# Another opening for a two-layer decoder trunk: the first two tiles' modulation on TensorE, c turned from eight rows

## The chip, the core and the metric

The kernel runs on one NeuronCore of a Trainium2 chip. Its engines are TensorE (PE, matrix products into PSUM; its weight loads are a row of their own, PEld), VectorE (DVE), ScalarE (ACT), GpSimd (POOL) and SyncE (SP, which only issues transfers). Each engine runs its own queue in order, and semaphores join them. The metric is the device time of one execution in microseconds (us); lower is better.

## The reference, cut to what matters

```python
def rmsnorm(x, g):                       # over the 1024 channels
    return x * rsqrt(mean(x * x) + EPS) * g

for i in range(2):                       # x is (256 tokens, 1024), c is (1024)
    mod = silu(c) @ w_ada[i] + b_ada[i]  # six pieces of 1024: shift, scale, gate, twice
    h = rmsnorm(x, norm_mix[i]) * (1 + sc1) + sh1
    x = x + g1 * mixer_i(h)              # i = 0: dilated attention, 1: gated linear attention
    h = rmsnorm(x, norm_ffn[i]) * (1 + sc2) + sh2
    x = x + g2 * conv_ffn(h)
return rmsnorm(x, norm_final)
```

The attention's first step is `h @ w_in` (1024 to 9216). Its scores get a learnt bias per distance (`rel_bias`), which the kernel calls position terms.

## The kernel before, in words

Channels lie on partitions: x is eight tiles (`kt`) of 128 channels by 256 tokens. Products keep near float32 precision by splitting each operand into a rounded high part and the rest: `whi`, `wlo` of weights (ACT copies the high part, `low_part` on DVE makes the rest) and `hhi`, `hlo` of h; each product is three (`hhi,whi`, `hlo,whi`, `hhi,wlo`).

The opening does this. c arrives as one row (`c_row`); PE multiplies it with a column of ones, so that it stands on all partitions, and ACT's Silu leaves it in `c_bc`. The squares of x are added on DVE and ACT, and PE's product with `ones_d` (tile `ms`) gives the mean for the norm (`rstd_of`). For each tile `kt` the loop at `w0, h = [], []` loads 128 rows of the modulation's weights twice over (`ada_load`), DVE takes two dot products with `c_bc` (`ada_dot`, tiles `dot`; L142), ACT adds the bias (`mod`), `normed` makes `hhi` and `hlo`, and `split` and `low_part` the parts of `w0[kt]`, the columns of `w_in` for the first two pairs of heads. PE then runs 36 products of 256 columns and 6 of 384 per tile into `pqk` and `pv` (L696, L700, L203 to L205). Products of the position terms (`rows`, L409) and warm-ups (`keep_warm`, results unused) stand before the first tile on PE.

The order on each engine follows `behind(...)` (issue after the named instructions) where it is written out, and a scheduler elsewhere. Loads go through SP in program order into four `raw` buffers, so a load can start when its buffer's last reader is done. After the first projection come the attention of eight pairs of heads (weights `wv`, `wqk`; bias rows read back from `rows_d`), its output, the FFN and the second layer; the change leaves them as they are.

```python
    rows_ps, at = [], 0
    with behind(norm_ops[0]):
        keep_warm(3)
...
            last_row = mm(ps, tab[:, 16 * g : 16 * g + 16], oh[:33, c], start=True, stop=True)
            at += n
    with behind(last_row):
        keep_warm(6)
```

## Time and profile before

| | us |
|---|---|
| median of 3 runs | 748.4 (748.07 to 750.87) |
| the profiled execution | 752.01 |
| its span, first to last instruction | 750.2 |
| PE busy in the span | 741.7 (99%) |
| DVE, ACT, POOL busy | 648.2, 480.6, 31.7 |
| mean granted clock of PE | 0.998 |

The span is what the trace covers; 1.8 us of the profiled execution lie around it. An engine's busy time counts an instruction from its start to its end, so overlapping products on PE count once. In the rows further down a line such as L142 is a line of the kernel, out<-in names tiles, and a bracket at the end tells how long the engine was idle before it and what released it.

### The profile page before, as it was taken

The page shows a single profiled execution, that of the slowest core. Times are in us where ns is not written, and L with a number is a line of the kernel's source. Part 1 is how long each engine was busy: PE and PEld are TensorE (multiplying, and loading weights), DVE is VectorE, ACT ScalarE, POOL GpSimd, SP SyncE. Part 2 cuts the span into 40 slices and gives each one's busy share as a digit, 9 for nine tenths or more (in the row PEclk, how much of TensorE's full clock was granted, in tenths as well). Part 3 has the DMA queues.
Part 4 walks back from the last instruction along what each step waited for, and adds up shares of the span by engine and source line. Part 5 has one row for each costly group of instructions (what it writes and reads, how often), then busy time and mean ns, then how long its engine had stood idle before and what let it go on. Part 6 is the DMA issues. An engine that isn't in the chain of part 4 may idle for free.

```text
span 750.2 us, 15928 instructions
## 1 busy us (share of the span) xinstructions
PE 741.7 (99%) x6344; PEld 726.6 (97%) x6344; DVE 648.2 (86%) x1195; ACT 480.6 (64%) x943; POOL 31.7 (4%) x57
## 2 busy tenths in 40 slices
PE   8999999999999999999999999999999999999997
PEld 5999999999999999999999999999999999999996
DVE  6997998989988859999998886898969999997592
ACT  5556775555656658776766565865768766666551
POOL 0002001101101010000000000000010000000100
PEclk9999999999999999999999999999999999999999
DMA  9998789888788438877746997776757766874621
GB/s 349 399 304 294 241 317 369 270 315 280 263 309 284 132 117 295 311 281 240 256 128 207 315 341 243 256 266 224 261 194 274 281 223 236 211 179 157 205 100 57
DMA packets 39481, 187.20 MB, mean 250 GB/s; under 512 B 9020, under 2 KB 11708, under 8 KB 25838
## 3 DMA queue, kind: packets, MB, share of 16 engines
q1 hardware_dynamic: 39024, 185.73, 71.4%
q8 instruction: 50, 0.82, 0.4%
q10 hardware_dynamic: 382, 0.45, 0.2%
q14 instruction: 25, 0.20, 0.1%
HBM read 185.06 MB, written 1.10 MB: 248 GB/s over the span
## 4 chain that ended last, share of the span: by engine, by line
PE 98%; DVE 1%; ACT 0%; DMA 0%; issue 0%; DVEq 0%; ACTq 0%
PE pab L204 10%; PE pab L205 10%; PE pab L203 10%; PE pqk L203 6%; PE pqk L205 6%; PE pqk L204 6%; PE pd L204 5%; PE pd L205 5%; PE pd L203 5%; PE pv L203 4%; PE pv L205 4%; PE pv L204 4%; PE pqk L696 2%; PE py L203 2%; PE py L205 2%; PE py L204 2%
## 5 line engine op out<-in xcount | busy, mean ns | idle before, releaser
L176 ACT CAST whi<-raw 128x1024 fp32r<-128x1024 f32 (+4 forms) x264 | 237.8, 945 | 107.0 <-PE pab L204 55.0
L182 DVE TENSOR_TENSOR wlo<-raw,whi 128x1024 fp32r<-128x1024 f32 (+5 forms) x248 | 263.8, 1092 | 30.6 <-ACT whi L176 29.8
L205 PE MATMUL pab<-hhi,wlo 128*128 128x256 f32 x672 | 185.0, 276 | 0.0
L204 PE MATMUL pab<-hlo,whi 128*128 128x256 f32 x672 | 184.9, 277 | 0.0
L203 PE MATMUL pab<-hhi,whi 128*128 128x256 f32 x672 | 183.1, 277 | 0.0
L204 PEld LDWEIGHTS pab<-hlo,whi 128*128 128x128 f32 x672 | 126.1, 188 | 0.2
L205 PEld LDWEIGHTS pab<-hhi,wlo 128*128 128x128 f32 x672 | 126.2, 188 | 0.0
L203 PEld LDWEIGHTS pab<-hhi,whi 128*128 128x128 f32 x672 | 125.1, 188 | 0.1
L142 DVE CUSTOM_DVE_ANT_0 ada_raw<-ada_raw,c_bc 128x1024 f32<-128x1024 f32 x96 | 114.3, 1230 | 4.6 <-DMA ada_raw<-in_w_ada 4.4
L203 PE MATMUL pqk<-hhi,whi 128*128 128x256 f32 x374 | 102.4, 279 | 0.0
L204 PE MATMUL pqk<-hlo,whi 128*128 128x256 f32 x374 | 101.8, 277 | 0.0
L205 PE MATMUL pqk<-hhi,wlo 128*128 128x256 f32 x374 | 101.3, 278 | 0.0
L205 PE MATMUL pd<-ghi,wlo 128*128 128x256 f32 x308 | 84.9, 276 | 0.0
L204 PE MATMUL pd<-glo,whi 128*128 128x256 f32 x308 | 84.9, 276 | 0.0
L203 PE MATMUL pd<-ghi,whi 128*128 128x256 f32 x308 | 84.7, 276 | 0.0
L203 PEld LDWEIGHTS pqk<-hhi,whi 128*128 128x128 f32 x374 | 69.9, 188 | 0.2
L204 PEld LDWEIGHTS pqk<-hlo,whi 128*128 128x128 f32 x374 | 69.9, 188 | 0.0
L205 PEld LDWEIGHTS pqk<-hhi,wlo 128*128 128x128 f32 x374 | 69.2, 188 | 0.1
L204 PEld LDWEIGHTS pd<-glo,whi 128*128 128x128 f32 x308 | 57.8, 188 | 0.0
L205 PEld LDWEIGHTS pd<-ghi,wlo 128*128 128x128 f32 x308 | 57.8, 188 | 0.0
L203 PEld LDWEIGHTS pd<-ghi,whi 128*128 128x128 f32 x308 | 57.7, 188 | 0.0
L204 PE MATMUL pv<-wlo,hhi 128*128 128x384 f32 (+2 forms) x160 | 52.8, 332 | 0.0
(272 smaller groups left out, 1440.8 us busy)
## 6 DMA issues: line engine op xcount, KB each, us to landing
raw<-in_w_up SPq DMA_DIRECT2D x42, 1024.0 KB, 4.9
ada_raw<-in_w_ada SPq DMA_DIRECT2D x29, 1024.0 KB, 6.0
raw<-in_w_down SPq DMA_DIRECT2D x28, 704.0 KB, 5.1
ada_raw<-in_w_ada SPq DMA_DIRECT2D x38, 512.0 KB, 6.8
raw<-in_wqk SPq DMA_DIRECT2D x18, 1024.0 KB, 6.7
raw<-in_wv SPq DMA_DIRECT2D x14, 768.0 KB, 7.0
raw<-in_w SPq DMA_DIRECT2D x7, 960.0 KB, 6.1
raw<-in_w_v_b SPq DMA_DIRECT2D x6, 768.0 KB, 5.0
```

Of the source, the lines that this page charges most:

```text
L142: i = dotted[0] = nc.vector.tensor_tensor_reduce(w, w, c_bc, op0=ALU.mult, op1=ALU.add, scale=1.0, scalar=0.0, accum_out=dot,)
L176: copied[0] = nc.scalar.copy(part(hi[:, c]), part(raw[:, c]))
L182: last_lo[0] = nc.vector.tensor_tensor(part(lo[:, c]), part(raw[:, c]), part(hi[:, c].bitcast(F32)), op=ALU.subtract)
L203: mm(ps, a[0], b[0], start=start, stop=False)
L204: mm(ps, a[0], b[1], start=False, stop=False)
L205: return mm(ps, a[1], b[0], start=False, stop=stop)
L696: mm(pqk[i], w[a], h[kt][b], start=s and i % 2 == 0 and (a, b) == (0, 0), stop=e and i % 2 == 1 and b == 1)
```

## The change

c is loaded as eight rows of 128, PE turns it (tile `ct`), and ACT's Silu puts it into column 0 of each 32-column block of a zeroed tile (`c_sel`). DVE and POOL each multiply four copies of the identity with four of these columns (`spread`), and a product with `ones_d` gives c on all partitions, which ACT copies to `c_bc`. For tiles 0 and 1 the modulation is now made by PE: eight products per tile, each with one block of `c_sel` as 32 columns of weights and 256 columns of `ada_first` passing through, in four column groups (`first_products`); DVE copies the four groups' sums out (`first_parts`), and two one-column products add them and turn them (`first_sums`). The position terms are six products of 128 columns in column groups of one bank. h's unrounded value of tiles 1 to 7 comes from `scaled_x` (x times the norm, on DVE for three and four tiles at once) and an ACT instruction. The two small tables `rel_bias` and `onehot` are loaded from POOL's queue. PE's order over the tiles is written out (`front`, `front_values`, `back`).

```diff
--- before.py
+++ after.py
-    c_row = wspl.tile([P, 2048], F32, tag="whi", name="c_row")
-    nc.scalar.dma_start(c_row[:1, :D], I["c"])
+    oh = wspl.tile([P, 2048], F32, tag="whi", name="oh")
+    c_sel, c_rows = oh[:, D + T : D + 2 * T].rearrange("p (k j) -> p k j", k=KT), oh[:KT, D : D + P]
+    nc.scalar.dma_start(c_rows, I["c"])
+    ident = const.tile([P, P], F32, name="ident")
+    make_identity(nc, ident)
+    nc.gpsimd.memset(c_sel, 0.0)
...
-    nc.scalar.dma_start(tab[:32, :], I["rel_bias"])
+    nc.gpsimd.dma_start(tab[:32, :], I["rel_bias"])
...
-    oh = wspl.tile([P, 2048], F32, tag="whi", name="oh")
-    nc.scalar.dma_start(oh[:33, :NROW], I["onehot"])
+    nc.gpsimd.dma_start(oh[:33, :NROW], I["onehot"])
...
     nc.vector.memset(eps, EPS)
-    ident = const.tile([P, P], F32, name="ident")
-    make_identity(nc, ident)
+    one = eps_one[:, 1:2]
+    nc.vector.memset(one, 1.0)
...
+    def keep_warm(n, tag="p"):
+        ps = bank("warm", tag)
+        for i in range(n):
+            last = mm(ps[:, :P], ones_d, ones_d, start=True, stop=True)
+        return last
     c_bc = const.tile([P, D], F32, name="c_bc")
-    for n in range(2):
-        ps = bank("cb", "t")
-        last_c = mm(ps, ones_d[:1, :], c_row[:1, 512 * n : 512 * n + 512], start=True, stop=True)
-        silu = nc.scalar.activation(c_bc[:, 512 * n : 512 * n + 512], ps, AF.Silu, scale=float(D))
+    first_warm = keep_warm(4)
+    nc.scalar.activation(eps_one[:, 2:3], one, AF.Silu)
+    c_turned = bank("ct", "s")
+    with behind(first_warm):
+        last_turn = nc.tensor.transpose(c_turned[:, 0:KT], c_rows, ident[:KT, :KT])
+    silu = nc.scalar.activation(c_sel[:, :, 0], c_turned[:, 0:KT], AF.Silu)
+    exp_ln_after(silu)
+    with behind(last_turn):
+        last_warm = keep_warm(4)
+    spread = wspl.tile([P, 2048], F32, tag="wlo", name="spread")
+    for n, engine in enumerate((nc.vector, nc.gpsimd)):
+        c = slice(512 * n, 512 * n + 512)
+        engine.tensor_tensor(spread[:, c].rearrange("p (k j) -> p k j", j=P),
+                             ident.unsqueeze(1).to_broadcast([P, 4, P]),
+                             c_sel[:, 4 * n : 4 * n + 4, 0:1].to_broadcast([P, 4, P]), op=ALU.mult)
+    c_ps = []
+    with behind(last_warm):
+        for n in range(2):
+            c_ps.append(bank("cb", "t"))
+            last_c = mm(c_ps[n], ones_d, spread[:, 512 * n : 512 * n + 512], start=True, stop=True)
+    with behind(last_c):
+        last_c = keep_warm(3)
...
+    def first_load(kt):
+        raw = wraw.tile([P, 2048], F32, tag="raw", name="ada_raw")
+        for c in (slice(0, D), slice(D, 2 * D)):
+            nc.sync.dma_start(raw[:, c], I["ada_first"][kt][:, c])
+        return raw
+    def first_products(raw, ps, ks, *after):
+        for k in ks:
+            j = slice(32 * (k % 4), 32 * (k % 4) + 32)
+            with behind(*after):
+                last = mm(ps[j, 0:T], c_sel[:, k, :], raw[:, T * k : T * k + T], start=(k < 4), stop=(k >= 4))
+        return last
+    def first_parts(ps, *after):
+        part = tmp.tile([P, T], F32, tag="sqacc", name="part")
+        with behind(*after):
+            i = nc.vector.tensor_copy(part, ps[:, 0:T])
+        return part, i
+    def first_sums(kt, ps, part, *after):
+        for i in range(2):
+            with behind(*after):
+                last = mm(ps[:, T + i : T + i + 1], part[:, P * i : P * i + P], one, start=True, stop=True)
+        return last, [modulation(0, piece, kt, ps[:, T + i : T + i + 1]) for i, piece in enumerate((1, 0))]
...
+    FIRST = 2
     sq = wspl.tile([P, 2048], F32, tag="wlo", name="sq").rearrange("p (k t) -> p k t", k=KT)
+    firsts = [first_load(0)]
+    for i in (0, 2):
+        nc.vector.tensor_tensor(sq[:, i : i + 2, :], x_all[:, i : i + 2, :], x_all[:, i : i + 2, :], op=ALU.mult)
+    last_add = nc.vector.tensor_tensor(sq[:, 0:2, :], sq[:, 0:2, :], sq[:, 2:4, :], op=ALU.add)
+    for i in (4, 6):
+        last_sq = nc.scalar.activation(sq[:, i : i + 2, :], x_all[:, i : i + 2, :], AF.Square)
+    with behind(last_add):
+        last_add = nc.vector.tensor_tensor(sq[:, 4:6, :], sq[:, 4:6, :], sq[:, 6:8, :], op=ALU.add)
+    with behind(last_sq):
+        for n in range(2):
+            last_copy = nc.scalar.activation(c_bc[:, 512 * n : 512 * n + 512], c_ps[n], AF.Copy, scale=float(D))
+    with behind(last_add):
+        last_terms = scale_terms(0)
+    mean, dots = bank("ms", "p"), bank("dots", "s")
     with behind(last_c):
-        keep_warm(4)
...
+        for i in (0, 1, 4, 5):
+            last_c = mm(mean[:, :T], ones_d, sq[:, i, :], start=(i == 0), stop=(i == 5))
+    for ks in (range(4), range(4, KT)):
+        last_c = first_products(firsts[0], dots, ks, last_c)
+    with behind(last_c):
+        last_warm = keep_warm(1)
...
+    part, last_part = first_parts(dots, last_terms)
+    def scaled_x(a, b, *after):
+        with behind(*after):
+            return nc.vector.tensor_tensor(all_early[:, a:b, 0:T], x_all[:, a:b, :],
+                                           r.unsqueeze(1).to_broadcast([P, b - a, T]), op=ALU.mult)
+    last_part = scaled_x(1, 4, last_part)
+    last_dots, last_mods = first_sums(0, dots, part, last_warm)
 
     rows_ps, at = [], 0
-    with behind(norm_ops[0]):
-        keep_warm(3)
-        for i, (g, n) in enumerate(ROWS):
-            c = slice(at, at + n)
-            ps = bank("rows", "t")[:16, 0:n]
+    row_bank = bank("rows", "t")
+    for i, (g, n) in enumerate(ROWS):
+        for first in range(0, n, P):
+            c = slice(at, at + P)
+            j = len(rows_ps)
+            ps = row_bank[32 * (j % 4) : 32 * (j % 4) + 16, P * (j // 4) : P * (j // 4) + P]
             rows_ps.append((ps, c))
-            last_row = mm(ps, tab[:, 16 * g : 16 * g + 16], oh[:33, c], start=True, stop=True)
-            at += n
-    with behind(last_row):
-        keep_warm(6)
+            with behind(last_dots):
+                last_row = mm(ps, tab[:, 16 * g : 16 * g + 16], oh[:33, c], start=True, stop=True)
+            at += P
...
+    def front(kt, terms, tiles=range(2 * NG), *after):
+        s, e = kt == 0, kt == KT - 1
+        for a, b in terms:
+            for i in tiles:
+                w = w0_parts(kt, P * i)
+                with behind(*after):
+                    last = mm(pqk[i], w[a], h[kt][b], start=s and i % 2 == 0 and (a, b) == (0, 0), stop=e and i % 2 == 1 and (a, b) == terms[-1])
+        return last
+    def front_values(kt, terms, *after):
+        s, e = kt == 0, kt == KT - 1
+        wv = w0_parts(kt, 6 * P, NG * P)
+        for a, b in terms:
+            for t in range(2):
+                with behind(*after):
+                    last = mm(pv[t][:, : NG * P], h[kt][a][:, P * t : P * t + P], wv[b], start=s and (a, b) == (0, 0), stop=e and (a, b) == BOTH[-1])
+        return last
+    def back(kt, tiles, *after):
+        for i in tiles:
+            with behind(*after):
+                last = mm3(pqk1[i], w0_parts(kt, 9 * P + P * i), h[kt], kt == 0 and i % 2 == 0, kt == KT - 1 and i % 2 == 1)
+        return last
...
     w0, h = [], []
-    last = last_add
+    last = last_part
     for kt in range(KT):
...
+        if kt >= FIRST:
+            ada = ada_load(0, kt)
+            with behind(last):
+                dots = [ada_dot(0, kt, 0, ada)]
+            with behind(dots[0][0]):
+                dots.append(ada_dot(0, kt, 1, ada))
+        elif kt:
+            firsts.append(first_load(kt))
+        if kt:
+            w0.append(split(I["w0"][kt], 15 * P, after=((), ()) if kt < FIRST else ((dots[0][1],), ()), lows=False))
+        else:
+            raw = wraw.tile([P, 2048], F32, tag="raw", name="raw")
+            for c in (slice(0, 960), slice(960, 1920)):
+                nc.sync.dma_start(raw[:, c], I["w0"][0][:, c])
+            whi = wspl.tile([P, 2048], F32R, tag="whi", name="whi")
+            wlo = wspl.tile([P, 2048], F32R, tag="wlo", name="wlo")
+            copied[0] = last_mods[1]
+            for c in (slice(0, 384), slice(384, 960), slice(960, 1920)):
+                with behind(copied[0]):
+                    copied[0] = nc.scalar.copy(whi[:, c], raw[:, c])
+            w0.append((whi, wlo, raw, 960))
+        hi, lo = h_hi[kt], h_lo[kt]
         if kt == 0:
+            a, sh = mod[0, 1, 0], mod[0, 0, 0]
+            hf = tmp.tile([P, T], F32, tag="xr", name="xr")
+            with behind(last):
+                nc.vector.scalar_tensor_tensor(hf, x[0], a[:, 0:1], r, op0=ALU.mult, op1=ALU.mult)
+            nc.vector.tensor_scalar(hi, hf, sh[:, 0:1], None, op0=ALU.add)
+            last = nc.vector.scalar_tensor_tensor(lo, hf, sh[:, 0:1], hi[:, :].bitcast(F32), op0=ALU.add, op1=ALU.subtract)
+            for i in range(2):
+                with behind(last):
+                    last = low_part(w0[0], i)
+            h.append((hi, lo))
             with behind(copied[0]):
                 for ps, c in rows_ps:
                     nc.scalar.copy(rows[:, c], ps)
+            done = front(0, ((0, 0), (0, 1)), range(2 * NG), last_row)
+            done = front_values(0, ((0, 0), (1, 0)), done)
+            continue
         if kt == 1:
+            done = first_products(firsts[1], second_ps, range(KT), done)
+            part, last = first_parts(second_ps, last)
+            last = scaled_x(4, KT, last)
+            done = front(0, ((1, 0),), range(2 * NG), done)
+            done = front_values(0, ((0, 1),), done)
+            done, _ = first_sums(1, second_ps, part, done)
+            done = back(0, range(6), done)
+        a, sh = mod[0, 1, kt], mod[0, 0, kt]
+        high = nc.scalar.activation(hi, early_x[kt][:, 0:T], AF.Identity, scale=a[:, 0:1], bias=sh[:, 0:1])
+        hf = tmp.tile([P, T], F32, tag="xr", name="xr")
+        with behind(high):
+            nc.scalar.activation(hf, early_x[kt][:, 0:T], AF.Identity, scale=a[:, 0:1], bias=sh[:, 0:1])
+        with behind(dots[1][0] if kt >= FIRST else last):
+            last = low_part(w0[kt], 0)
+        with behind(last):
+            last = nc.vector.tensor_tensor(lo, hf, hi[:, :].bitcast(F32), op=ALU.subtract)
+        chain[kt] = chain[7] = high, last
+        with behind(last):
+            last = low_part(w0[kt], 1)
+        h.append((hi, lo))
+        if kt == 2:
             with behind(last):
                 last = scale_terms(1)
+        done = front(kt, BOTH, range(2 * NG), done)
+        done = front_values(kt, BOTH, done)
+        done = back(kt, range(6), done)
...
-    A["c"] = a["c"]
+    A["c"] = a["c"].reshape(KT, P)
...
+    first = np.stack([np.concatenate([wa[0, :, p, k, :] for p in (1, 0)], axis=1) for k in range(2)])
+    A["ada_first"] = first.reshape(2, KT, P, 2 * P).transpose(0, 2, 1, 3).reshape(2, P, 2 * D)
```

On PE, at the start of the program, before the change (tiles as above; x counts equal instructions in a row):

```order
L125 MATMUL cb<-c_row,ones_d 128x512 x2
L301 MATMUL warm<-ones_d 128x128 x4
L215 MATMUL ms<-sq,ones_d 128x256 x2
L301 MATMUL warm<-ones_d 128x128 x3
L409 MATMUL rows<-oh,tab 16x512
L409 MATMUL rows<-oh,tab 16x128 x2
L301 MATMUL warm<-ones_d 128x128 x6
L696 MATMUL pqk<-hhi,whi 128x256 x6
```

and on PE at the same place after it:

```order
L138 MATMUL warm<-ones_d 128x128 x4
L146 MATMUL ct<-ident,oh 128x8
L138 MATMUL warm<-ones_d 128x128 x4
L161 MATMUL cb<-spread,ones_d 128x512 x2
L138 MATMUL warm<-ones_d 128x128 x3
L454 MATMUL ms<-sq,ones_d 128x256 x4
L206 MATMUL dots<-ada_raw,oh 32x256 x8
L138 MATMUL warm<-ones_d 128x128
L218 MATMUL dots<-eps,part 128x1 x2
L482 MATMUL rows<-oh,tab 16x128 x6
L499 MATMUL pqk<-hhi,whi 128x256 x6
```

Warm-ups moved from behind the position terms to the places around c, and the modulation's products (`dots`) stand between the mean and the first projection product.

On POOL, after the constants of the program's start, after the change (before it the identity's two instructions had only four small fills around them):

```order
masks.py:197 MEMSET ident 128x128
L98 MEMSET oh 128x256
L108 DMA tab<-in_rel_bias 32x48
L110 DMA oh<-in_onehot 33x768
masks.py:199 ISA
masks.py:199 AFFINE_SELECT ident<-ident 128x128
L808 MEMSET q 128x16
L808 MEMSET q 128x8
L826 MEMSET k 128x4 x2
L154 TENSOR_TENSOR spread<-ident,oh 128x512
```

A fill and two transfers now stand ahead of the instruction that completes the identity, and half of `spread` is new.

On SP, after the load of the last tile's projection weights, after the change (before it the two `wv` loads stood together, ahead of all loads of `bias`):

```order
L234 DMA raw<-in_wv 128x1536
L428 DMA bias<-rows_d 64x258
L429 DMA bias<-rows_d 64x2x64
L428 DMA bias<-rows_d 64x258
L429 DMA bias<-rows_d 64x2x64
L428 DMA bias<-rows_d 64x258
L429 DMA bias<-rows_d 64x2x64
L428 DMA bias<-rows_d 64x258
L429 DMA bias<-rows_d 64x2x64
L234 DMA raw<-in_wv 128x1536
L234 DMA raw<-in_wqk 128x2048 x2
```

The second half of the first value weights moved behind eight small loads.

## Rows read from the trace of the kernel before

**Rows 1.** The page: busy us (share of the span) and instructions of each engine.
```profile
PE 741.7 (99%) x6344; PEld 726.6 (97%) x6344; DVE 648.2 (86%) x1195; ACT 480.6 (64%) x943; POOL 31.7 (4%) x57
```

**Rows 2.** Waits of PE, whole span: us in total, times, longest.
```profile
PE cb L125 <- DMA c_row<-in_c: 3.0, 1, 3.0
```

**Rows 3.** Stretches: busy us (instructions) of PE, PEld, DVE, ACT, POOL; granted clock, DMA share, GB/s.
```profile
17.30:22.30 5.00, 5.00 (x32) 5.00 (x32) 4.95 (x8) 2.53 (x5) 0.00 (x0) 1.00 1.01 418
...
100.00:740.00 640.00, 639.85 (x5585) 631.29 (x5584) 558.16 (x1025) 416.87 (x817) 25.42 (x35) 1.00 0.70 241
...
23.73:60.70 36.97, 36.97 (x297) 36.97 (x295) 32.81 (x51) 20.52 (x40) 1.58 (x4) 1.00 0.92 329
```

**Rows 4.** Timeline of PE, opening: start us, duration us, engine, line, operation.
```profile
6.63 2.08 PE L301 MATMUL warm<-ones_d 128*128 128x128 f32 x8
...
12.05 2.74 PE L409 MATMUL rows<-oh,tab 33*16 33x512 f32 x6
...
14.72 2.93 PE L301 MATMUL warm<-ones_d 128*128 128x128 f32 x12
...
17.30 1.63 PE L696 MATMUL pqk<-hhi,whi 128*128 128x256 f32 x6
...
20.20 0.87 PE L696 MATMUL pqk<-hlo,whi 128*128 128x256 f32 x6
...
23.73 0.87 PE L696 MATMUL pqk<-hhi,whi 128*128 128x256 f32 x6
...
64.91 0.51 PE L203 MATMUL pv<-whi,hhi 128*128 128x384 f32 x2
```

**Rows 5.** Timeline of ACT's own queue of transfers, opening.
```profile
1.68 0.44 ACTq L96 DMA_DIRECT2D tab<-in_rel_bias  x1
```

**Rows 6.** Timeline of ACT, opening.
```profile
11.70 0.37 ACT L150 ACTIVATE mod<-dot,one_b,small 128x1 f32<-128x1 f32 x1
...
12.17 0.97 ACT L176 CAST whi<-raw 128x960 fp32r<-128x960 f32 x1
13.05 0.50 ACT L289 ACTIVATE hhi<-xr,mod 128x256 fp32r<-128x256 f32 x1
```

**Rows 7.** Timeline of DVE, opening.
```profile
9.47 1.22 DVE L142 CUSTOM_DVE_ANT_0 ada_raw<-ada_raw,c_bc 128x1024 f32<-128x1024 f32 x1
...
12.11 0.48 DVE L287 SCALAR_TENSOR_TENSOR xr<-x_all,mod,rstd 128x256 f32<-128x256 f32 x1 [0.26 <-ACT mod L150]
13.17 1.16 DVE L188 TENSOR_TENSOR wlo<-raw,whi 128x960 fp32r<-128x960 f32 x1 [0.58 <-ACT whi L176]
...
20.00 1.16 DVE L188 TENSOR_TENSOR wlo<-raw,whi 128x960 fp32r<-128x960 f32 x1
```

**Rows 8.** Timeline of DVE and POOL, two sums of squares on POOL.
```profile
271.52 1.29 DVE L198 TENSOR_TENSOR wlo<-raw,whi 128x512 fp32r<-128x512 f32 x2
...
272.13 1.29 POOL L230 TENSOR_TENSOR sqacc<-sq 128x256 f32<-128x256 f32 x1 [37.29 <-ACT sq L227]
273.49 0.74 POOL L230 TENSOR_TENSOR sqacc<-sqacc,sq 128x256 f32<-128x256 f32 x1
```

**Rows 9.** Transfers of x, first modulation weights, tile 1's projection weights: issue, us to landing.
```profile
L92 SPq DMA_DIRECT2D x_all<-in_xR x2: 389/406/422, 0.7 to 1.2; - x2
...
DMA to landing us min/median/max: 4.3/4.8/5.3
...
L135 SPq DMA_DIRECT2D ada_raw<-in_w_ada x2: 424/626/829, 1.7 to 2.1; - x2
...
DMA to landing us min/median/max: 7.0/7.4/7.7
...
L169 SPq DMA_DIRECT2D raw<-in_w x1: 433/433/433, 6.9 to 6.9; - x1
...
DMA to landing us min/median/max: 10.2/10.2/10.2
```

**Rows 10.** Timeline of PE, attention: products in two column groups of 64.
```profile
101.90 1.08 PE L591 MATMUL po<-pt,v 128*64 128x256 f32 x8
```

82 lines of the change are left out of this document (26 added, 56 removed).

## The prediction

> **What bounds the kernel now.** I read the page first: TensorE (PE) is busy 741.7 of 750.2 us [rows 1]. Then the waits of PE: only one is listed, 3.0 us at the very start for the vector c [rows 2]. Then the busy time by stretches: from 100 to 740 us PE has 639.85 of 640, and over the seven tiles that follow the first one (23.73 to 60.70) all 36.97, so a tile of the first projection costs 36.97 / 7 = 5.28 us [rows 3]. Nothing after the opening waits, so only the moment at which PE begins its second tile, 23.73, can move the end.
>
> The timeline of PE then shows what fills the time before 23.73 [rows 4]. It is not waiting but filler, at half pace: twelve warm-up products start at 14.72, the first six projection products at 17.30 take 1.63 us, six like them at 20.20 take 0.87. So PE passes from the lower to the higher of its clock levels (1.2 and 2.4 GHz) between 18.9 and 20.2, say at 19.6. The granted clock column says 1.00 for all of 17.30 to 22.30 [rows 3]; the spacing of the products is what tells the levels apart here. Before that rise PE ran full-width products from 14.72 without a break, some 4.9 us. Earlier full-width work (from 6.63 on, eight warm-ups and the sums of squares) was followed from 12.05 by position terms on 33 rows and 16 columns, and brought no rise. VectorE (DVE) is no bound at tile 1: PE begins it at 23.73, DVE's operands for it were done by 21.16 [rows 7].
>
> **The change, part by part.** I follow one chain to the start of PE's first projection product, now 17.30.
>
> *c in eight rows.* It must land (PE's wait ended at 2.96 [rows 2]) and be turned with the identity. GpSimd (POOL) now fills c's zero block (an estimated 0.3) and issues two DMAs ahead of finishing the identity. The trace has no DMA issued by POOL. The nearest row is ScalarE's (ACT's) issue, 0.44 [rows 5]; as upper bound I take 1.5 each, between three and four times that. I take 0.9: the identity is ready at 3.4 (2.5 to 4.6). By the Trainium skill's page "DMA: Bandwidth & Descriptors" (Specifications) a DMA from GpSimd has about 1 us to its first byte against about 0.6 from ACT; by that alone the issue would cost 0.4 more than ACT's, and the identity come at 3.2. Turning and Silu cost an estimated 0.8 with their hand-overs (the nearest ACT row, one column, is 0.37 [rows 6]): 4.2.
>
> *The spread.* DVE's half is a two-input product of 512 columns; two such take 1.29 [rows 8], so 0.65: 4.85. POOL's half: 256 columns take 0.74 when DVE reads nothing beside it [rows 8], so about 1.35 for 512. But the same instruction took 1.29 from 272.13 on, where the second of two such DVE products ran until 272.81 [rows 8]: POOL stood still until DVE was through. So I put POOL's half behind DVE's, done at 6.2, and DVE's squares of x (first half landed at 5.0, second at 6.5 [rows 9]) behind POOL's: their sums come at about 8.9 instead of 7.9. The Trainium skill, "SBUF — State Buffer" (Who interferes with whom), says that two-input DVE work and a POOL instruction that reads SBUF exclude each other for a whole instruction; the trace agrees, and by that rule the sum is the same. Were the two to run side by side, the squares would be ready a microsecond earlier, at little gain, since PE comes to them no sooner than 8.35.
>
> *PE up to the modulation.* At the low level a 128-column product spaces at 0.213 per instruction, two instructions each (eight in 2.08 less the tail [rows 4]). Four warm-ups follow the turn (3.5 to 5.2), two c products of 512 columns (four times 0.43; the second waits for POOL) end at 7.1, three warm-ups at 8.35. The four mean products are eight instructions of 0.43 at the low level or 0.213 at the high one. When does the clock rise? PE is now on full-width work from 3.5 with at most a break of 1 us before 6.2. The one rise that the trace has came after some 4.9 us of such work without a break; the same here gives 8.4 if the short break is nothing and 11.1 if all counts from its end. I take 9.0. Then the mean is through at 10.5. The modulation products (eight, in four column groups) need their weights, landed at 8.6 and 9.8 [rows 9]: no wait. Their price: in the attention, eight instructions of 256 columns in two column groups take 1.08 us [rows 10], four slots of 0.21 plus a tail; sixteen in four groups take four slots too, 0.85. They end at 11.35, with the tail 11.5.
>
> *From there to the first product:* DVE copies the sums (0.45, like its other passes over 256 columns [rows 7]), PE adds the groups (two one-column products, estimated 0.6), ACT makes the modulation 0.4, DVE scales x 0.48 and makes the high part 0.45 [rows 6, 7]: 11.5 + 2.4 = 13.9. DVE's scaling of three other tiles fits beside it. The position terms (now six short products in column groups) lie between the sums and 13.9 and cost nothing; without that cover, 0.5. ACT's cut of the first weight conversion to 384 columns (half of 0.97) lets six products start before all is converted. So PE starts at 13.9 instead of 17.30.
>
> *Tile 0* then has 5.28 of projection, 0.85 for the second tile's modulation and 0.35 for its sums: 13.9 + 6.5 = 20.4. Now it takes 6.43, as its first 2.5 us are slow. PE begins tile 1 at 20.4 instead of 23.73: **3.3 us earlier**.
>
> *What caps it.* Tile 1 needs its projection weights. They are issued at 6.9 and land 10.2 later, at 17.1 [rows 9], and the same bytes stand ahead of them after the change. ACT then converts two halves (0.9 each), makes two modulations (0.6 together) and the high part (0.5) [rows 6]: 20.0. More than 3.7 us can't be had unless transfers run faster.
>
> *Later tiles.* DVE loses one product of 0.48 per tile (ACT makes the unrounded value, one more 0.5 there): two dot products of 1.22, two low parts of 1.16 and 0.45 [rows 7], less their overlaps of 0.08, make 4.9 against PE's 5.28, so DVE keeps ahead. Transfers of 2.03 MB per tile (128 rows of 2048 and 1920 columns) take 4.9 us at the 418 GB/s of the stretch from 17.30 [rows 3]; just enough. ACT has about 3.6 per tile. One DMA moves: the second half of the value weights is now issued by SyncE behind eight bias loads; at 0.44 or more per issue [rows 5] that is 4 to 5 us later in that queue. PE first touches it at 64.91 [rows 4], 61.6 after the change; issued near 52 and landing 5 to 7 us later, it has 1 to 2 us to be converted. I take no loss, bound 1 us.
>
> **Sum.** 3.3 us off the profiled execution (752.0 becomes 748.7, its span 746.9) and off the median, 748.4, which is 3.6 below the profiled one; I take the opening to be the same in both. That gives **745.1 us**, 0.44% down. About 0.5% (3.7 us) is what a measurement of this kernel tells from no change, so the forecast is "within 0.5%", close to its edge.
>
> **The rivals.**
> 1. *The clock does not rise in time.* If the break before 6.2 or the waits around the column sums count, PE stays at the low level: mean until 11.75, modulation products 1.7 instead of 0.85, first projection product at 16.1, and with the rise at 19.6 as now tile 0 ends near 24.3, about 0.6 later than today: 749.0; with a rise at 12, 746.7. For it: the stretch from 6.63 to 12.05 brought no rise [rows 4]. Against: the new work is at full width throughout. The Trainium skill, "TensorE: Matmul & The Clock Gate" (Part 1), has the low level as the default that sustained activity releases; the trace agrees on that, and leaves open whether a short break counts. Chance 0.17.
> 2. *POOL is late.* With 1.5 us per DMA issue the identity comes 1.2 later and the whole chain with it: 746.3; were the one-hot rows to land after 13.9, they would hold up every product behind them. Chance 0.12.
> 3. *The opening gains more.* If DVE and ACT hand over quicker and the first transfers (fewer small packets in ACT's queue) land up to 1 us earlier, tile 1 starts at 19.4 or before: 743.4 to 744.5. Chance 0.13.
> 4. *Slower: column groups of 32 run one after another.* Then each set of modulation products costs 3.4 instead of 0.85 at the high level, 2.55 twice: 3.3 becomes a loss of 1.8, 750.2, and 752.7 if the first set runs at the low level. It decides the sign where four groups gain less than 1.4 times over one. The pairs of [rows 10] speak against it. Chance 0.05.
> 5. *Given back later*, at the value weights: 746 to 748. Chance 0.03.
>
> **How the numbers follow.** The forecast (2.3 to 3.9 gained, 744.5 to 746.1) has 0.50. The range goes from 743.5, the far end of rival 3, to 747.9, between the late rises of rival 1; what lies beyond (half of rival 1, part of 2 and 3, all of 4) has 0.2. Faster by over 0.5% is below 744.7: rival 3 and the best third of the forecast, 0.31. Slower by over 0.5% is above 752.1: part of rival 4 and what I have not seen, 0.05. The rest, 0.64, is within 0.5%.
>
> **What would show it.** In the profile after: warm-ups before c lands; POOL's half spread ending near 6.2 and DVE's squares beginning behind it; product spacing falling from 0.213 to 0.11 near 9; the eight modulation products within about 1 us; the first projection product near 13.9, tile 1 near 20.4, with ACT's conversions of its weights starting at 17.1. I am wrong if the spacing stays low past 12, if POOL's issues take over 1.5, if the groups run in line, or if PE waits again between 25 and 70.

## The result, and the profile after

The changed kernel takes 751.78 us (median of ten runs, 750.04 to 753.22), the kernel before 748.30 beside it: the ratio is 1.0038, 95% interval 1.0022 to 1.0054. It is slower, by 2.9 us between the means and 3.5 between the medians, where 3.3 us less were forecast. Medians and ratios here and below leave out the few executions over 1.5% longer than the fastest of their kernel (775.83 us is one).

The profiled execution is the longest of the ten (753.22 us, span 751.4), so its waits are above the usual. The line of TensorE (PE) and its neighbours that answers to [rows 1]:

```profile
PE 739.1 (98%) x6393; PEld 725.1 (96%) x6393; DVE 643.7 (86%) x1186; ACT 485.0 (65%) x955; POOL 35.0 (5%) x61
```

PE's waits over the whole span, where [rows 2] had one line:

```profile
PE pqk L499 <- ACT hhi L571: 3.8, 3, 2.2
PE warm L138 <- DVE eps L121: 1.2, 1, 1.2
PE pqk L499 <- ACT whi L542: 1.0, 1, 1.0
PE pqk L268 <- ACT v L795: 0.4, 1, 0.4
...
```

The first line is new and lies between 25 and 51 us: three times PE waits for ACT's high part of h. The timeline of PE shows where (start, duration; compare [rows 4]):

```profile
3.40 1.86 PE L138 MATMUL warm<-ones_d 128*128 128x128 f32 x8
5.10 1.88 PE L161 MATMUL cb<-spread,ones_d 128*128 128x512 f32 x4
6.82 0.83 PE L138 MATMUL warm<-ones_d 128*128 128x128 f32 x6
...
9.38 1.07 PE L206 MATMUL dots<-ada_raw,oh 128*32 128x256 f32 x16
...
13.12 0.94 PE L499 MATMUL pqk<-hhi,whi 128*128 128x256 f32 x6 [0.97 <-ACT whi L542]
...
20.04 0.84 PE L499 MATMUL pqk<-hhi,whi 128*128 128x256 f32 x6
25.94 0.97 PE L499 MATMUL pqk<-hhi,whi 128*128 128x256 f32 x6 [0.54 <-ACT hhi L571]
31.33 0.97 PE L499 MATMUL pqk<-hhi,whi 128*128 128x256 f32 x6
37.84 0.97 PE L499 MATMUL pqk<-hhi,whi 128*128 128x256 f32 x6 [1.02 <-ACT hhi L571]
43.17 0.94 PE L499 MATMUL pqk<-hhi,whi 128*128 128x256 f32 x6
50.86 0.97 PE L499 MATMUL pqk<-hhi,whi 128*128 128x256 f32 x6 [2.22 <-ACT hhi L571]
56.34 0.97 PE L499 MATMUL pqk<-hhi,whi 128*128 128x256 f32 x6
```

The opening goes about as forecast. The clock is up at 5.10: from there four instructions of 512 columns take 1.88 us, and at 6.82 six idle ones of 128 take 0.83, where eight took 2.08 at the low level [rows 4]. The sixteen modulation products take 1.07, the projection starts at 13.12 instead of 17.30 and tile 1 at 20.04 instead of 23.73. But tile 7 starts at 56.34; in the profile before it starts at 55.44. Tiles 1 to 6 take 36.30 us, 6.05 a tile, where PE needs 5.28 [rows 3].

What PE waits for ahead of tile 6 (its first product at 50.86) is seen on ACT, then on DVE:

```profile
47.81 0.99 ACT L241 CAST whi<-raw 128x960 fp32r<-128x960 f32 x1 [4.23 <-DMA raw<-in_w]
48.71 0.38 ACT L190 ACTIVATE mod<-dot,one_b,small 128x1 f32<-128x1 f32 x1
49.00 0.97 ACT L241 CAST whi<-raw 128x960 fp32r<-128x960 f32 x1
49.88 0.29 ACT L192 ACTIVATE mod<-dot,small 128x1 f32<-128x1 f32 x1
50.20 0.60 ACT L571 ACTIVATE hhi<-early_x,mod 128x256 fp32r<-128x256 f32 x1
50.71 0.59 ACT L574 ACTIVATE xr<-early_x,mod 128x256 f32<-128x256 f32 x1
```

```profile
47.32 0.08 DVE L179 DVE_READ_ACCUMULATOR2_ANT dot<- 128x1 f32 x1
50.01 1.16 DVE L253 TENSOR_TENSOR wlo<-raw,whi 128x960 fp32r<-128x960 f32 x1 [2.60 <-ACT whi L241]
51.33 0.43 DVE L578 TENSOR_TENSOR hlo<-xr,hhi 128x256 fp32r<-128x256 f32 x1 [0.17 <-ACT xr L574]
51.67 1.15 DVE L253 TENSOR_TENSOR wlo<-raw,whi 128x960 fp32r<-128x960 f32 x1
```

ACT's first step for the tile is the cast of the second half of the projection weights. It waits 4.23 us for their landing, and both modulations, whose dot products were ready at 46.2 and 47.4, stand behind it in ACT's order. So does the high part of h. Over tiles 2 to 7 ACT waits 14.6 us for landings in six places. The weights for tile 6 were issued only at 39.88, when DVE's second low part for tile 4 had freed their buffer:

```profile
38.66 1.15 DVE L253 TENSOR_TENSOR wlo<-raw,whi 128x960 fp32r<-128x960 f32 x1
```
```profile
39.88 0.33 SPq L234 DMA_DIRECT2D raw<-in_w  x1
```

### The profile page after: what moved, and what is told of

Same layout as the page of the kernel before. It is cut to its first block, busy times and chain, and to the rows that moved or that the text cites. A ratio compares the mean times of both kernels' runs of the same rounds, so it can differ in the third digit from the quotient of the medians.

```text
span 751.4 us, 16040 instructions
## 1 busy us (share of the span) xinstructions
PE 739.1 (98%) x6393; PEld 725.1 (96%) x6393; DVE 643.7 (86%) x1186; ACT 485.0 (65%) x955; POOL 35.0 (5%) x61
## 4 chain that ended last, share of the span: by engine, by line
PE 82%; DVE 6%; DMA 6%; ACT 4%; issue 1%; DVEq 0%; ACTq 0%; SPq 0%
PE pab L269 10%; PE pab L270 10%; PE pab L268 10%; PE pqk L268 5%; PE pqk L270 5%; PE pqk L269 5%; PE pd L268 4%; PE pd L269 4%; PE pd L270 4%; DMA raw<-in_w 3%; PE pv L269 2%; PE pv L270 2%; PE pv L268 2%; PE py L268 2%; ACT whi L241 2%; PE py L269 2%
## 5 line engine op out<-in xcount | busy, mean ns | idle before, releaser
L241 ACT CAST whi<-raw 128x1024 fp32r<-128x1024 f32 (+5 forms) x262 | 236.1, 945 | 127.6 <-PE pab L269 55.3
L179 DVE CUSTOM_DVE_ANT_0 ada_raw<-ada_raw,c_bc 128x1024 f32<-128x1024 f32 x92 | 109.4, 1229 | 3.1 <-DMA ada_raw<-in_w_ada 3.0
L268 PE MATMUL pqk<-hhi,whi 128*128 128x256 f32 x374 | 104.4, 279 | 0.4 <-ACT v L795 0.4
L270 PE MATMUL pqk<-hhi,wlo 128*128 128x256 f32 x374 | 103.8, 278 | 0.1
L269 PE MATMUL pqk<-hlo,whi 128*128 128x256 f32 x374 | 103.7, 277 | 0.0
```

What stands on the lines that cost most here:

```text
L179: i = dotted[0] = nc.vector.tensor_tensor_reduce(w, w, c_bc, op0=ALU.mult, op1=ALU.add, scale=1.0, scalar=0.0, accum_out=dot,)
L241: copied[0] = nc.scalar.copy(part(hi[:, c]), part(raw[:, c]))
L268: mm(ps, a[0], b[0], start=start, stop=False)
L269: mm(ps, a[0], b[1], start=False, stop=False)
L270: return mm(ps, a[1], b[0], start=False, stop=stop)
```

## The experiments

The theories, by the letters that the expectations use. **A**: the four raw buffers delay the loads. **B**: ACT's order in the new loop body (cast of the second half, modulation, cast of the first half, modulation, high part) is the loss. **C**: DVE together with ACT paces the stage at 5.3 to 5.4 us a tile, so an earlier start of PE only brings waits. **D**: the second value load, now behind eight bias loads on SyncE (SP), costs 0.6 us. **E**: the profiled execution of the kernel before was not its usual one. **F** and **G**: the new loop body costs by itself, or does not. "Before" is the kernel before on the same chip, 747.8 to 748.0 us in every set.

**e1, more places for the modulation weights.**
```diff
-            ada = ada_load(0, kt)
+            ada = ada_halves(kt)      # halves 0..3 in w30, w31, w32 and one pt place
```


> The changed kernel, with the modulation weights of tiles 2 to 7 in four half places of 4 KB (three of them used later for the attention's modulation, one for a later tile), so that the four raw buffers are left to the projection weights. Theory A (a load is issued only when an old tile frees its buffer, lands 6 to 8 us later, and two tiles take 11.8 us where TensorE needs 10.6): the second and later projection loads are issued some 5 us earlier, TensorE's waits ahead of tiles 2, 4 and 6 (0.7, 1.2 and 2.4 us) go to under 0.5 us in all, and the time falls by 3.5 to 4.3 us to about 747.6 us, 0.999 of the kernel before. Theory B (ACT's order: both modulations and the high part of h stand behind the cast of the second half, which waits for its landing): casts in the same order, so the chain of casts, modulations and high part still ends some 2 us late in each tile; the time stays within 0.7 us of 751.8 us.

754.25 us, ratio 1.0077 (1.0053 to 1.0100). The loads are issued earlier, but ACT's order had changed with it (modulation, both casts, modulation, high part, float32 copy), contrary to what I wrote there. ACT, and VectorE's product that waits for its copy:

```profile
36.69 0.39 ACT L190 ACTIVATE mod<-dot,one_b,small 128x1 f32<-128x1 f32 x1 [2.71 <-DVE dot L179]
36.99 1.88 ACT L241 CAST whi<-raw 128x960 fp32r<-128x960 f32 x2
38.77 0.29 ACT L192 ACTIVATE mod<-dot,small 128x1 f32<-128x1 f32 x1
```
```profile
34.02 0.43 DVE L597 TENSOR_TENSOR hlo<-xr,hhi 128x256 fp32r<-128x256 f32 x1 [1.06 <-ACT xr L593]
...
40.22 0.43 DVE L597 TENSOR_TENSOR hlo<-xr,hhi 128x256 fp32r<-128x256 f32 x1 [1.06 <-ACT xr L593]
```
Here the weights have landed, ACT waits for DVE's dot products and DVE for ACT's copy: 6.20 us a tile, and from tile 3 on ACT waits for no transfer. So a body can lose without any late landing. What freed buffers are worth in the changed kernel's own order (A), this run does not tell.

**e2, modulations and high part first on ACT, then both casts.**
```diff
+        for c in (slice(0, 960), slice(960, 1920)) if kt >= FIRST else ():
+            with behind(copied[0]):      # behind the float32 copy of h
+                copied[0] = nc.scalar.copy(w0[kt][0][:, c], w0[kt][2][:, c])
```


> The changed kernel with one order changed on ACT for tiles 2 to 7: both modulations, the high part of h and its float32 copy come first, then the casts of the first and the second half (now: second half, modulation, first half, modulation, high part). Theory B: from a tile's landing to TensorE's first product goes from 3.1 us to about 1.0 us, and to the release of its buffer from 5.0 to about 3.6 us; TensorE's waits ahead of tiles 2, 4 and 6 fall from 4.3 us to under 0.5 us, time about 747.6 us. Theory A: the buffers still set when loads are issued; only what the order takes off the path is won, about half of the waits, 749.5 us.

762.09 us, ratio 1.0176 (1.0142 to 1.0210): worse than either theory had it. The casts now stand behind the dot products, and DVE, which needs the first cast, waits each time:

```profile
34.09 1.16 DVE L255 TENSOR_TENSOR wlo<-raw,whi 128x960 fp32r<-128x960 f32 x1 [2.37 <-ACT whi L579]
```
DVE's steps and ACT's follow one another, about 7.2 us a tile (tiles 6 and 7 start at 55.77 and 62.99). My repair was wrong; that ACT's order sets the pace, it shows.

**e3, a later start.**
```diff
+    for _ in range(28):
+        with behind(last_row):
+            last_row = mm(mean[:, T : T + P], ones_d, ones_d, start=True, stop=True)
```


> The changed kernel with 28 idle products (about 3.0 us at 0.107 us) ahead of the first product of the projection, so that TensorE starts it 3 us later. Theories A and B agree: VectorE, ACT and the loads keep their pace whatever TensorE does, so the waits ahead of tiles 2, 4 and 6 shrink by the same 3 us and the time stays within 0.5 us of 751.8 us. The rival, that the time between the start of the projection and the end is fixed and the loss lies somewhere else: 754.8 us.

758.06 us, ratio 1.0121 (1.0088 to 1.0153). I had the size wrong: each such product is two instructions, 56 in 6.52 us, so the start moved by 6.4 us:

```profile
13.25 6.52 PE L522 MATMUL ms<-ones_d 128*128 128x128 f32 x56
```
Tile 7 starts at 59.57, 3.2 us later than in the changed kernel's profile, but the median is 6.3 us above the changed kernel's: nearly all of the delay comes through, which is nearest to the rival. The premise was wrong as well. Tile 1's modulation products stand inside tile 0's projection on PE and moved from 15.37 to 21.78, and with them DVE's dot products for tile 2, from 21.65 to 27.56. So the edit delayed DVE, ACT and the loads too, and does not separate the theories.

**e4, both value loads ahead of the first pair's bias loads.**
```diff
-        if u == 0:
-            with tc.issue_after(last_load[0].ins):
-                bias = load_bias(0)
+            with tc.issue_after(last_load[0].ins):      # at u == 1, behind the value loads
+                bias = load_bias(0)
```


> The changed kernel with the first pair's eight bias loads moved behind both loads of the value weights on SP (the second is issued at 58.6 us, behind the bias loads, before the change at 48.5 us). Theory D: the wait of 0.58 us at 71.5 us is due to this order, and the time falls by 0.4 to 0.6 us to about 751.3 us. Theories A and B say nothing of it; if the copies of the values set that wait by themselves, the time does not change.

752.02 us, ratio 1.0050 (1.0034 to 1.0066): no gain. The wait ahead of 72.1 us is gone, but the waits for the high part (3.4 us in five places, in the longest of the ten executions) hide what that is worth. D is no cause of the loss by itself.

**e5, the kernel before once more.** No edit.

> The kernel before, unchanged, once more, for a profile. Its times lie in two groups, 747.2 to 748.4 us (three quarters) and 750.9 to 751.7 us, and the execution that was profiled first is of the second (752.01 us; clock up at 19.6 us, first product of the projection at 17.30 us behind idle products of 0.213 us). Theory E: in the first group the clock is up earlier, before the row products at 12.05 us, so that these and the six idle products run at 0.11 us and the projection starts 2.5 to 3.3 us earlier, near 14.0 to 14.8 us; the change then saves about 1 us at this place and not 4.2. If this execution is of the second group again, it shows the same as before. Rival: the first group has the same opening and is faster elsewhere.

748.56 us, span 746.8, and the timeline of PE is another one than [rows 4]:

```profile
10.67 0.83 PE L301 MATMUL warm<-ones_d 128*128 128x128 f32 x6
11.43 1.47 PE L409 MATMUL rows<-oh,tab 33*16 33x512 f32 x6
12.83 1.60 PE L301 MATMUL warm<-ones_d 128*128 128x128 f32 x12
14.19 0.95 PE L696 MATMUL pqk<-hhi,whi 128*128 128x256 f32 x6
19.56 0.87 PE L696 MATMUL pqk<-hhi,whi 128*128 128x256 f32 x6
...
46.45 0.97 PE L696 MATMUL pqk<-hhi,whi 128*128 128x256 f32 x6
51.82 0.97 PE L696 MATMUL pqk<-hhi,whi 128*128 128x256 f32 x6
```
The six idle products take 0.83 us at 10.67, the twelve at 12.83 take 1.60 (2.93 at 14.72 before): the clock is up by 10.7 us, after the same products. The projection starts at 14.19, not 17.30. E holds for this execution; of the kernel before, 17 of 104 executions in all sets are of the longer kind (above 750.4 us). Busy times from tile 1 to tile 7 of this execution, then of the changed kernel (PE, PEld, DVE, ACT, POOL; clock, DMA share, GB/s):

```profile
19.56:51.82 32.26, 32.13 (x254) 31.79 (x253) 31.57 (x50) 16.81 (x31) 0.00 (x0) 1.00 0.99 382
```
```profile
20.04:56.24 36.20, 32.41 (x254) 31.66 (x252) 29.32 (x43) 20.58 (x37) 0.00 (x0) 1.00 0.89 321
```
In its usual execution the kernel before has DVE busy for 98% of this stage, beside 99.6% of PE. From tile 1 to tile 5 the tiles follow each other at PE's 5.29 to 5.31 us; then DVE has no lead left, and the next two come after 5.70 and 5.37.

**e6 and e7, the kernel before with early idle products, and then without the nine idle ones ahead of the projection.**
```diff
+    first_ps = bank("warm", "t")                    # e6 and e7, ahead of the c products
+    for i in range(4):
+        first_warm = mm(first_ps[:, :P], ones_d, ones_d, start=True, stop=True)
-        keep_warm(3)                                # e7 only
-    with behind(last_row):
-        keep_warm(6)
```


> The kernel before with four more idle products (8 passes) from 1.2 us on, ahead of the products that spread c, so that TensorE works from 1.2 us without a long pause. Theory E: the clock is up by 7 us in every run, the first product of the projection comes near 14.0 to 14.8 us, and all times lie near 748 us, none near 751.5; ratio 0.998 to 1.000. Rival: the clock has no part in the two groups; a quarter of the runs stays at 751.5 us.

> As the last kernel, and without the nine idle products ahead of and behind the row products, which stand between the reciprocal root and the projection (18 passes of 0.107 us at the fast clock, 1.9 us). Theory C (VectorE and ACT give a tile every 5.3 to 5.4 us, TensorE takes 5.28, so that the end of the eight tiles is theirs and an earlier start only brings waits): less than 0.5 us below the last kernel. Rival, the prediction's own step: the earlier start is kept, up to 1.3 us below it (the first high parts are ready near 13 us).

e6: 748.69 us (747.98 to 749.13 in ten runs, none near 751.5), ratio 1.0000 (0.9987 to 1.0013). No execution is of the upper group, as E says, but that is a weak sign: 4 of 23 are beside it, so one or two of ten were to be expected, and in e16's set none of eleven of the kernel before is. The other half of E missed: in the profiled execution the clock was not up by 7 us (eight idle products still took 2.08 at 6.91), and PE starts only at 15.27; yet the span is 746.9. e7: 748.77, ratio 1.0018 (1.0008 to 1.0027): no gain, as C says, but its clock fell again after a wait of 1.8 us (its first six projection products took 1.65 us), so it is no clean test.

**e8 and e9, the old loop body for tiles 2 to 7 in the changed kernel; e9 with e4's load order too.**
```diff
+                w0.append(split(I["w0"][kt], 15 * P, after=((dots[0][1],), (high,)), lows=False))
+            h.append(normed(0, 0, r, kt, (dots[1][0],), between))
```


> The changed kernel with the old body of the loop for tiles 2 to 7 (x times scale and rstd on VectorE again, ACT: modulation, first half's cast, modulation, high part, second half's cast); the opening and tiles 0 and 1 stay changed. Theory F (the new body is what loses: in it ACT's five steps and VectorE's two low parts of a tile follow one another, and a late landing is passed on whole): VectorE runs without pause from 21.7 us in 5.38 us a tile, ends tile 7 near 54 us as before (now 58.2), TensorE's waits at tiles 2 to 6 fall under 1.5 us, time 748.0 to 748.5 us. Theory A (buffers and landings alone): the waits stay above 3.5 us, 751 to 752 us.

> The last kernel (changed opening, old loop body for tiles 2 to 7) with the first pair's bias loads behind both value loads as well. In the last kernel TensorE lost 0.5 us at 62.7 and 1.4 us at 68.9 us, in the stretch where the second value load (issued behind the bias loads) is split. Theory F and D together (loop body and load order are what the change loses by): both waits go, the time falls from 750.9 to 748.8 to 749.2 us, 1.001 to 1.002 of the kernel before: the opening's 1.1 us at the first product is not kept, since tile 1 begins at 20.0 us (19.6 before). Rival: other waits take their place, 750.5 to 751 us.

e8: 750.30 us, ratio 1.0033 (1.0007 to 1.0058), above F's 748.0 to 748.5. The waits for the high part fall from 3.8 us to 0.2, as F says. But PE now comes to the second value load too early: 1.2 us for the values' copies and 0.4 for their low part take their place, and little is won. e9: 750.52, ratio 1.0024 (1.0010 to 1.0039). Its profiled execution (748.94 us, one of the shortest) has no wait between tile 1 at 20.82 and tile 7 at 52.48.

**e10, TensorE makes tile 0's modulation alone** (old body for tiles 1 to 7, e4's load order).
```diff
-    FIRST = 2
+    FIRST = 1
```


> As the last kernel, but with TensorE making the modulation of tile 0 alone; tile 1 goes through the loop as before (its two dot products on VectorE), and x times rstd is no longer made ahead. TensorE saves the products and sums of tile 1's modulation, about 1.2 us between 15.4 and 18 us. Theory C (VectorE's 5.38 us a tile and the landings pace the stage): tile 1 starts near 19.5 us with a wait of about 1 us ahead of it, the end of the eight tiles is VectorE's as before; 747.7 to 748.3 us, the time of the kernel before within 0.3 us. Rival (the early start is kept once TensorE is relieved): 746.8 us.

748.58 us, ratio 1.0002 (0.9987 to 1.0017): the kernel before again, by the ratio. The timeline of PE:

```profile
13.08 0.94 PE L498 MATMUL pqk<-hhi,whi 128*128 128x256 f32 x6 [0.97 <-ACT whi L557]
18.94 0.98 PE L498 MATMUL pqk<-hhi,whi 128*128 128x256 f32 x6 [0.36 <-ACT hhi L346]
24.77 0.97 PE L498 MATMUL pqk<-hhi,whi 128*128 128x256 f32 x6 [0.27 <-ACT hhi L346]
30.23 0.97 PE L498 MATMUL pqk<-hhi,whi 128*128 128x256 f32 x6
35.61 0.96 PE L498 MATMUL pqk<-hhi,whi 128*128 128x256 f32 x6
...
51.76 0.97 PE L498 MATMUL pqk<-hhi,whi 128*128 128x256 f32 x6
```
This is C in one view: PE starts at 13.08, waits ahead of tiles 1 and 2, then follows DVE at 5.38 us, and tile 7 starts at 51.76. Over tiles 2 to 7 ACT waits 14.3 us for DVE's dot products and 0.4 for a landing. Starts at 13.08, 14.19 (e5) and 15.27 (e6) give tile 7 at 51.76, 51.82 and 52.35, and spans of 746.8, 746.8 and 746.9 (single executions; those of one kernel differ by half a microsecond and more).

**e11, the changed kernel once more.** No edit.

> The changed kernel once more, for a second profile: the one that was profiled is the longest of ten executions (753.22 us, median 751.78). Theory A: in a shorter one the landings of the tiles come earlier against TensorE, waits ahead of tiles 2 to 6 of about 3 us where the first showed 4.3; first product at 13.1 us in both. Rival: the executions differ in the opening, by when the clock rises.

750.87 us, span 749.1: tile 1 at 20.65, waits for the high part 1.7 us in two places, tile 7 at 54.69. The opening is the same, the landings differ, as A has it.

**e12, the kernel before with one more DVE product per tile.**
```diff
+                xi = nc.vector.scalar_tensor_tensor(twice, x[kt], a[:, 0:1], r, op0=ALU.mult, op1=ALU.mult)
```


> The kernel before with one more VectorE instruction in each of tiles 1 to 7 (x times scale and rstd once more into a place that nobody reads, 0.48 us, 0.40 as spaced: 2.8 us in seven tiles). Theory C (VectorE paces the stage without slack worth speaking of, in the usual execution where the projection starts at 14.2 us): TensorE gets waits ahead of the later tiles, the time rises by 2.0 to 2.8 us to 750.0 to 750.8 us. Rival (VectorE is ahead by most of a tile, as the prediction read it from the execution with the late start): the time rises by less than 0.5 us.

749.39 us, ratio 1.0022 (1.0010 to 1.0033): 1.4 us of the 2.8 added come through (0.7 to 2.5 by the interval). So DVE had some slack over the seven tiles, about 1.4 us, less than the rival and more than I gave it; no profile shows where it lay. The profiled execution (751.48 us) is one with the late start at 17.30; there nothing waits and tile 7 starts at 55.35, as in the first profile. That is the slack that the prediction read.

**e13 and e16, the new loop body where only tile 0 is TensorE's; and e10 with one cast moved.** e13 is the changed kernel with FIRST = 1 and e4's load order. e16 is e10 with one edit:
```diff
-                w0.append(split(I["w0"][kt], 15 * P, after=((dots[0][1],), (high,)), lows=False))
+                w0.append(split(I["w0"][kt], 15 * P, after=((dots[0][1],), ()), lows=False))
```


> As e10 (changed opening for tile 0 alone, values first), but with the changed kernel's loop body for tiles 1 to 7 (x times rstd made ahead, the high part of h and its copy on ACT, the second half's cast first on ACT). Theory F (the new body is slower by itself: a late landing holds up all five ACT steps of a tile): 749.7 to 750.5 us, 1 to 2 us above e10's 748.6, with waits for the high part ahead of several tiles. Theory G (the body costs nothing where VectorE's stream is not set back by tile 1): within 0.4 us of e10.

> As e10 (old loop body, tile 0 alone on TensorE, 748.6 us), with one order changed on ACT in tiles 1 to 7: the cast of the second half comes first, ahead of the modulations, as in the changed kernel (in e10: modulation, first half's cast, modulation, high part, second half's cast). Theory B: this place of the cast is what the new body loses by, since the modulations and the high part then wait for the landing of the projection weights: 750 to 751.5 us, with waits of TensorE for the high part of 2 us and more in all between tile 2 and tile 7. Rival: the loss comes from the work moved to ACT (the float32 copy of h); then within 0.5 us of 748.6, or below it, since the second low part no longer waits for its cast.

e13: 751.33 us, ratio 1.0047 (1.0027 to 1.0066), 4.7 us of waits for the high part in four places (in an execution of 753.96). e16: 752.69, ratio 1.0074 (1.0059 to 1.0090), 4.1 us above e10. Its ACT ahead of tile 4, then PE:

```profile
34.87 1.00 ACT L241 CAST whi<-raw 128x960 fp32r<-128x960 f32 x1 [3.64 <-DMA raw<-in_w]
35.77 0.38 ACT L190 ACTIVATE mod<-dot,one_b,small 128x1 f32<-128x1 f32 x1
36.06 0.98 ACT L241 CAST whi<-raw 128x960 fp32r<-128x960 f32 x1
```
```profile
37.83 0.97 PE L498 MATMUL pqk<-hhi,whi 128*128 128x256 f32 x6 [1.06 <-ACT hhi L346]
```
In e10 the modulation for this tile ran at 33.44, before ACT touched the new weights. The place of this one cast is enough to lose what the change lost: B holds, in this form. The profile is of e16's shortest execution (750.18 us); it has 1.5 us of waits for the high part between tiles 2 and 7, under the 2 expected, 1.3 more at tile 1, and tile 7 at 53.79, 2.0 later than e10. The rest of the 4.1 lies in executions that were not profiled.

**e14, e9 once more.** No edit.

> e9 again, for a profile of another of its executions (they lie from 748.4 to 753.1 us, and the one profiled took 748.94 us and has no wait ahead of a tile). Theory C (VectorE's stream has no slack after tile 1's late end): this one, if it takes 750 us or more, has waits for the high part or a low part of 1 us and more in all between 20 and 70 us, where a landing came later. Rival: it loses in the opening, by a clock that rises later.

749.49 us, again without a wait ahead of a tile (tile 7 at 52.20); it loses 0.3 us at the values and 1.1 near the end of the program. Neither answer: e9's executions of 751 us and more were not caught.

**e15, e10 with work moved from DVE to GpSimd (POOL).**
```diff
+    for a, b in ((1, 3), (3, 5), (5, KT)):
+        nc.gpsimd.tensor_tensor(all_early[:, a:b, 0:T], x_all[:, a:b, :], ...)
+            nc.gpsimd.tensor_scalar(hf, early_x[kt][:, 0:T], a[:, 0:1], sh[:, 0:1], op0=ALU.mult, op1=ALU.add)
```


> As e10, with 0.4 us a tile less on VectorE: x times rstd is made ahead on GpSimd, GpSimd makes the float32 h that VectorE needs for the low part, ACT the high part straight from x times rstd; ACT's order as in the kernel before. Theory C: tiles 2 to 7 follow each other at TensorE's 5.28 us rather than at 5.38, the waits ahead of tiles 3 to 7 (0.1 us each) and part of those at tiles 1, 2 and in the values (1.6 us in all) go; 747.0 to 747.8 us, 0.998 to 0.999 of the kernel before. Rival (GpSimd's work stretches VectorE's, as the 1.50 us for a product of 512 columns beside it showed, 1.29 alone; or the landings set the pace): 748.2 to 749 us.

752.12 us, ratio 1.0044 (1.0023 to 1.0066). It fails in the opening: POOL's three products (11.41 to 15.87) run beside DVE's chain for tile 0.

```profile
11.41 4.46 POOL L472 TENSOR_TENSOR early_x<-x_all,rstd 128x512 f32<-128x512 f32 x3 [6.01 <-ACT rstd L462]
```
```profile
12.95 1.24 DVE L573 SCALAR_TENSOR_TENSOR xr<-x_all,mod,rstd 128x256 f32<-128x256 f32 x1 [1.08 <-ACT mod L190]
14.30 1.72 DVE L574 TENSOR_SCALAR hhi<-xr,mod 128x256 fp32r<-128x256 f32 x1
```
The first of these takes 0.48 alone [rows 7]. PE starts at 16.17. The 1.50 and 1.29 us that the expectation names are for two products each. The question of DVE's pace is left to e10 and e12.

## Why the prediction was wrong

**Up to tile 1 the steps held.** "c in eight rows" and "The spread": the turn came at 3.20, POOL's two issues took 0.70 and 0.55 (0.9 each assumed), POOL's half ended at 5.40 (forecast 6.2). "PE up to the modulation": the clock was up by 5 us, not 9; four column groups ran side by side, sixteen instructions in 1.07 us (forecast 0.85 and a tail), so rival 4 is out. "From there to the first product": 13.12 against 13.9. Three terms were estimates with no row behind them: the zero block 0.3, turn and Silu 0.8, the group sums 0.6; they took 0.32, 0.6 and 0.61. "Tile 0": 6.92 us instead of 6.5, tile 1 at 20.04 against 20.4. Rivals 1 and 2 did not occur. That the total came so near is partly luck: 0.43 for 512 columns is the price at the high level (by the same paragraph's 0.213 for 128 the low level asks 0.85), and it fitted only because the clock rose 4 us earlier than assumed. POOL's half took 1.55 us beside DVE's 0.69, and ended 0.9 after it, not 1.35 as put.

**"Sum" failed first.** "I take the opening to be the same in both" is the sentence. The profiled execution lay 3.6 us above the median, and the reason lay in the very stretch that the change replaces: a clock that rose at 19.6 us. In the one profile of the usual kind it is up by 10.7 and tile 1 starts at 19.56 (e5). Against that the change begins the projection 1.07 us earlier, spends 1.55 more on tile 0 (the second tile's modulation: 1.07 of products and 0.50 of sums), and is 0.48 late at tile 1. The 3.3 us were never to be had from the median: tile 1 comes 3.69 us earlier only against the execution whose clock rose late.

**"Later tiles" failed second.** I added up DVE's instructions to 4.9 us a tile and called it ahead of PE. But DVE and ACT hand over to each other several times in a tile, and ACT's order decides whether they run in parallel. In the old body DVE runs without a break at 5.37 to 5.38, 0.1 us slower than PE at 5.28. In the new one DVE waits 0.36 us for ACT even in a tile that no landing holds up (5.30 us, from 39.73 to 45.03); in others ACT's first step waits for a landing, and everything behind it is late.

The lateness feeds itself, and so A has its part beside B. "Transfers ... just enough" took a rate, but a tile's load is issued when DVE's second low part of two tiles earlier frees the buffer. For tile 6 it was issued at 39.88, landed 7.9 us later, and from there to the end of the tile's second low part (52.82) took 5.0: 12.9 us for two tiles. In e10 the same way takes 10.75 (37.66 to 48.41), at most 6.9 to the landing and 3.8 behind it. Of the 2.2 us, some 1.2 are the order of the steps and 1.0 the longer landing, which no run explains. By the two profiles, against e5: start −1.07, tile 0 +1.55, tiles 1 to 6 36.30 instead of 32.26, +4.04; together 4.52 us, and the spans differ by 4.6. For e11 the same sum is −0.79 + 1.88 + 1.78 = 2.87 (spans: 2.3). The two enclose the 3.5 us between the medians.

The medians of the four combinations, all with values first, show how the two parts share it:

| | new body | old body |
|---|---|---|
| tiles 0 and 1 on TensorE | 752.0 (e4) | 750.5 (e9) |
| tile 0 alone | 751.3 (e13) | 748.6 (e10) |

The body costs 1.5 to 2.7 us, tile 1's modulation on TensorE 0.7 to 1.9 (the intervals leave each median about 1 us). For the second the traces suggest two sides, though neither profile with it and the old body (e9, e14) shows a wait ahead of a tile: PE's 1.55 us, and DVE's dot products for tile 2, which start at 21.65 in the changed kernel (21.16 before), because tile 1's chain runs over ACT behind both casts of weights that land at about 17 in either kernel. How the 1.9 splits between them was not tried apart. "What caps it" saw the landing, and not that it caps DVE's whole later stream too. "Given back later" (rival 5) had the right kind of end and the wrong place; the value weights matter only once the tiles no longer wait (e8).

No version here beats the kernel before. By the ratios e6 and e10 equal it; their medians lie 0.7 and 0.6 us above its own, and they had no execution of the longer kind.

## What to carry to other kernels

If the profiled execution is longer than the median by as much as the change is to gain, find out first what it does differently there; a second profile is cheap. An engine that is busy for 98% of a stage beside the "bound" one can be the bound too: here starts 2.2 us apart (e10, e6) ended in spans 0.1 us apart. On an engine that runs in order, put no step that waits for a transfer ahead of steps whose operands are ready: moving one cast of 1 us cost 4.1.

## What the runs showed of the hardware

- The same kernel, with the same products on TensorE ahead of it, had the clock up by 10.7 us in one execution (e5) and at 19.6 in another (and in e12's, whose PE order is the same up to there); with idle products from 1.2 us on (e6, e10, the changed kernel) no profile had a rise later than 13. After a rise it was low again in two profiles, each time behind a wait of PE: 1.8 us in e7, 3.1 us in e15. Behind a wait of 1.0 in the changed kernel it was still up. The granted clock column reads 1.00 for 17.30 to 22.30, whose first 2.3 us lie before the rise [rows 3]; of the later fall in e15 it tells (0.50, the third figure from the end):

```profile
13.80:20.50 6.70, 4.33 (x18) 4.36 (x19) 6.56 (x8) 3.21 (x10) 2.07 (x2) 0.50 0.81 309
```

- POOL's products stretched two DVE instructions to 1.24 and 1.72 us in e15, each ending 0.15 to 0.3 us after one of POOL's did; the second reads a single large tile and one column. The Trainium skill, "SBUF — State Buffer" (Who interferes with whom), says that a DVE instruction with two SBUF inputs, or one in a mode that uses both ports, and a POOL instruction that reads SBUF exclude each other; the trace agrees for the first, and whether the second ran in such a mode no run shows.
